# First expert pass in blocks of 128 neighbouring rows, its map built inside the pass, low parts of the tokens subtracted by VectorE inside it

## The chip, the cores and the metric

One core of one Trainium2 chip. The time is device microseconds of one execution of the whole program; a run is compared by its median over several executions. Before the change it is 1549.99 us, the median of 3 runs from 1548.42 to 1551.87.

## What is computed

A trunk of two layers on 512 tokens of width 1024, in f32. Each layer runs a token mixer (layer 0 a Conformer convolution module of 31 taps, layer 1 a short gated convolution of 3 taps) and then a hierarchical mixture of experts. Each of the two sub-layers is wrapped as

```
h = x * (1 + scale(c)) + shift(c)
x = LayerNorm(ALPHA * x + (1 + gate(c)) * sublayer(h))
```

with scale, shift and gate from a matrix product of a conditioning vector c. The mixture of experts chooses for each token one of 4 groups and in it the best 2 of 8 experts, and sums their weighted outputs; an expert is

```
hid = silu(x @ w_gate) * (x @ w_up)        # 1024 -> 512
y   = hid @ w_down                         # 512 -> 1024
```

There are 32 experts a layer, 6 MB of weights each. The choice needs full f32 precision, so the mixers' products are made of a high part and a low part of each operand (`mm3`: high by high, high by low, low by high).

## The kernel before, in words

**Weights.** All large weights come through a ring of 6 SBUF tiles of 2 MB (`R`, `RING`), in the order of the list `todo`. `pump` issues the next tile's DMAs on SyncE's queue, `unit()` hands out the oldest tile, and `done()` gives one back and pumps; a tile's DMAs wait on the chip until the instructions that read its predecessor are through. The expert weights follow each other by pass; the numbers of the experts of pass 1 and later are read from `ids`, which the routing writes. Pass 0 uses experts 0 and 1 whatever the routing says, so its weights can come ahead of it.

**Passes.** Layer i's experts run in 14 passes (`PASSES`), each with 128 token slots, split among 1 to 4 experts; pass 0 has two experts with 64 slots each. In a pass (from L1239's loop) `t` runs over 16 steps: step t multiplies 128 rows of the gathered tokens, block k, with the gate (z = 0) or the up weights (z = 1). Before, four blocks of the gate come first, then four of the up, and again. After steps 3, 7, 11 and 15 `release` gives tiles back. Then come `silu`, the product, a transposition, and eight steps with the down weights. f32 matmuls show as two instructions each.

**Gather.** Tokens reach their slots by a matmul with a one-hot matrix (`gather`, L1005 for pass 0, L1011 for the later ones). It makes two blocks k at a time; ScalarE evicts the even one and VectorE the odd one (L1014, L1016), with the map of the adaLN scale and shift (`affe`, `offe`) in the same instruction. `u_pass` gives partition p the rows 8p to 8p + 7 of a weight matrix, in two halves of four rows (runs of 8 KB). So block k of a pass consists of the columns k, k + 8, k + 16, ... of X: a step of eight elements. For pass 0 the gather reads X itself with that step as its weights. For the later passes it reads `nh` and `nl`, the high and the low parts of X in the permuted order, which are made just after the router's logits (L933, by `split`): ScalarE copies each of the four blocks of 128 tokens to `nh` (L461), and GpSimd subtracts for `nl` (L462).

**The permuted map.** `affine` (L443 to L445) makes `aff` and `off`, 128 neighbouring channels a column. `fold_router` adds the router's bias from `off` (L254), and builds the map in the order of the passes, `aff8`: an iota on GpSimd (L259), seven small instructions on VectorE (L260 to L266), eight matmuls (L269) and a copy on ScalarE (L272). Its inner `finish` adds the bias to `rb` and scales the router's weights `rw` (L275, L276). It is called in both mixers ahead of the output product: in layer 0 between the convolution's moments (`moments`, L722, L725) and their use (L816 to L822, spread over all channels by L831, applied in `conv_norm`, L839, L840); in layer 1 after the last weight product of the mixer and before the output product, whose weights `Out.fold` scales on GpSimd (L531) and splits on ScalarE and VectorE (L533, L539).

**Order.** The schedule is written by hand: each engine runs its instructions in the order of the program text, GpSimd too, and waits only for data and buffers. `W` hands out one of 21 tiles of 2 KB a partition, `P` one of 8 PSUM banks in three groups ("a" 4, "b" 2, "c" 2). Between the router's logits (L891) and pass 0 VectorE chooses the experts (`choose`, L905 to L923: a round of five steps for the group and the best expert together, then a round for the second best), TensorE counts (L938 to L946), and the ranks, the places and the one-hot of pass 0 follow (L950 to L1060). `flex` and, in layer 0, `side_ada` are modulation products whose last steps stand in this stretch and at step 3 of pass 0 (L366, L381, L384, L389).

Of the kernel before, what the change touches and what calls it, by code (L numbers as in the profile page):

```python
# [62 lines left out]
def trunk_kernel(ctx: ExitStack, tc: tile.TileContext, x, c, ada_w, ada_b, a_w_in, a_b_in, a_w_dw, a_b_dw,  # L63
# [114 lines left out]

    def u_last(i, d):
        def f():  # L180
            n = len(PASSES[-1])
            t = R([128, n, 2, 512])
            for s, e in enumerate(experts(i, NP - 1)):
                nc.sync.dma_start(t[:, s], e_w_down[i, e].rearrange("o (p h k) n -> h p (o k) n", h=2, k=2)
                                  [1][:, :, d * 512:(d + 1) * 512])
            return t
        return f
# [9 lines left out]
    for i in range(DEPTH):  # L197
        if i == 1:
            todo += [u_bin(nb) for nb in range(2)]
            for nb in range(2, KD):  # L200
                todo += [u_ada1(1, 1 + nb // 2, nb % 2), u_bin(nb)]
        else:
            todo += [rest.popleft()]
        todo += [u_out((a_w_out, b_w_out)[i][0], h) for h in range(2)]
        todo += list(rest) if i == 0 else []
        todo += [u_ada1(1, v, kq) for v in ((1, 0), (5,))[i] for kq in range(2)]
        for g in range(NP):
            n = len(PASSES[g])
            if g < NP - 1:
                todo += [u_pass(i, g, j) for j in range(3 * n)]  # L210
            else:
                todo += [u_pass(i, g, j) for j in range(5 * n // 2)] + [u_last(i, d) for d in range(2)]
# [38 lines left out]
    def fold_router(i, rw, aff, off):  # L251
# [3 lines left out]

        u, spread8 = W([128, 512]), W([128, KD, 2, 8])
# [11 lines left out]
        for k in range(KD):  # L268
            PE.matmul(p[:, 64:80], div8[:, 112 - 16 * k:240 - 16 * k], spread8[:, k].rearrange("p z j -> p (z j)"),  # L269
                      start=k == 0, stop=k == KD - 1)  # L270
        aff8[i] = T([128, 2, 8], F32, "aff8")
        S.activation(aff8[i].rearrange("p z j -> p (z j)"), p[:, 64:80], AF.Copy)  # L272

        def finish():
            V.tensor_add(rb[:, i, :], rb[:, i, :], p[:, :NG + NE])  # L275
            V.tensor_mul(rw, rw, bc(aff[:, :, None], [128, KD, NG + NE]))  # L276
# [34 lines left out]
    aff8 = {}  # L311
# [540 lines left out]
    for i in range(DEPTH):  # L852
# [77 lines left out]

        for q in range(NQ):
            qs = slice(q * 128, (q + 1) * 128)
            split(nh[:, :, qs], nl[:, :, qs], X[:, q, :].rearrange("p (n k) -> p k n", k=KD), G)  # L933
# [65 lines left out]
        def gather(Q, k0):  # L999
            p = P("c", (128, 2, 256))  # L1000
            n = 128 if Q % (NP // 2) == 0 else 256
            for k in (k0, k0 + 1):
                for q in range(NQ):
                    if Q == 0:
                        PE.matmul(p[:, k - k0, :n], X[:, q].rearrange("p (n k) -> p k n", k=KD)[:, k], oh(Q, q), start=q == 0, stop=q == NQ - 1)  # L1005
                        continue
# [3 lines left out]
                    for part, src in enumerate((nh, nl)):  # L1010
                        PE.matmul(p[:, k - k0], src[:, k, q * 128:(q + 1) * 128], o, start=q == 0 and part == 0,  # L1011
                                  stop=q == NQ - 1 and part == 1)
            k = k0
# [4 lines left out]
        affe, offe = aff8[i][:, 0], aff8[i][:, 1]  # L1018
# [106 lines left out]
        def block(e, rest, eid, tiles):  # L1125
# [6 lines left out]
            for h, xt in enumerate((xa, xb)):  # L1132
# [8 lines left out]
                for b in range(4):  # L1141
                    PE.transpose(p[:, b, :], xt[:, b * 128:(b + 1) * 128], ident)
                for b in range(4):
# [62 lines left out]
        for g, kind in enumerate(PASSES):  # L1206
# [27 lines left out]
            for t in range(2 * KD):  # L1234
                z, k = t // 4 % 2, t // 8 * 4 + t % 4
                if t % 4 == 0:
                    w = [piece(t // 4 * ns + s) for s in range(ns)]
                for s, a, b in cols:
                    PE.matmul(pgu[z][a:b, :], xe(Q, k, j)[:, a:b], w[s][:, t % 4, :], start=k == 0, stop=k == KD - 1)  # L1239
# [12 lines left out]
                if g == 0:  # L1252
                    if t in (0, 4, 6):
                        gather(0, {0: 2, 4: 4, 6: 6}[t])
# [276 lines left out]
```

## Time and profile before

| what | value |
| --- | --- |
| median of 3 runs | 1549.99 us |
| profiled execution, its own time | 1551.05 us |
| its span in the trace | 1548.9 us |
| TensorE busy | 1431.8 us, 92% |
| weight loads of TensorE (beside matmuls) | 785.4 us, 51% |
| VectorE busy | 726.0 us, 47% |
| ScalarE busy | 341.4 us, 22% |
| GpSimd busy | 283.9 us, 18% |
| DMA of the ring's queue | 486.82 MB, 79.2% of 16 engines |
| mean rate from HBM | 314 GB/s over the span |

Matmuls overlap each other in the pipeline, so a busy TensorE is not one at its peak. Layer 0's mixer ends at about 265 us, its experts at about 767 us; layer 1's mixer ends at about 1010 us. In the rows further down PE is TensorE, PEld its weight loads, DVE VectorE, ACT ScalarE, POOL GpSimd and SPq SyncE's queue of DMAs; L12 is line 12 of the kernel before.

### The profile page before, as it was taken

To read this page: it belongs to the slowest core of one execution; us is meant where nothing else is said; L and a number is where in the kernel's file an instruction comes from. 1 tells how busy PE (TensorE), PEld (TensorE's weight loads), DVE (VectorE), ACT (ScalarE), POOL (GpSimd) and SP (SyncE) were. 2 spreads that over 40 slices of the span, in tenths; PEclk is the share of its full clock that TensorE was granted. 3 is DMA by queue.
4 is the path that set the end of the run, shared out by engine and by line. 5 is a ranking of instruction groups with operands and counts; after the bars stand their busy time and mean duration, and the time that the engine had idled before them with its cause. 6 is when DMAs were issued, how large, how long until landed. Compare 5 with 4: busy or idle time off the path is not lost. (4 is left out here: it accounts for less than half of the span.)

```text
span 1548.9 us, 21328 instructions
## 1 busy us (share of the span) xinstructions
PE 1431.8 (92%) x8424; PEld 785.4 (51%) x8424; DVE 726.0 (47%) x1290; ACT 341.4 (22%) x583; POOL 283.9 (18%) x283
## 2 busy tenths in 40 slices
PE   5999888798999999998899898979899999999975
PEld 3444467553545444543277776856354444445422
DVE  2799887442333333333157876552433333333214
ACT  1456365120011101101052222232110111001001
POOL 1399923223000000000024105020500000000002
PEclk8999989899999999999899998989999999999988
DMA  8954424489999999999994673237999999999984
GB/s 296 396 184 169 161 88 184 164 313 422 421 394 403 389 421 421 421 420 418 360 303 150 196 243 131 101 123 304 365 422 415 407 405 400 421 421 420 420 358 172
DMA packets 112453, 488.73 MB, mean 316 GB/s; under 512 B 11971, under 2 KB 45259, under 8 KB 63179
## 3 DMA queue, kind: packets, MB, share of 16 engines
q1 hardware_dynamic: 108043, 486.82, 79.2%
q8 instruction: 71, 1.16, 0.3%
q0 software_dynamic: 128, 0.04, 0.2%
q10 hardware_dynamic: 4160, 0.30, 0.2%
q14 instruction: 51, 0.42, 0.1%
HBM read 485.02 MB, written 2.10 MB: 314 GB/s over the span
## 5 line engine op out<-in xcount | busy, mean ns | idle before, releaser
L1239 PE MATMUL pa<-ring,w 128*32 128x512 f32 (+2 forms) x2624 | 433.2, 607 | 25.8 <-DMA ring<-in_e_w_up_dram 12.1
L1239 PEld LDWEIGHTS pa<-ring,w 128*32 128x32 f32 (+2 forms) x2624 | 119.2, 120 | 275.7 <-issue 244.6
L1113 DVE TENSOR_TENSOR X<-X,pb 128x512 f32<-128x512 f32 x208 | 133.8, 683 | 265.8 <-PE pb L1121 259.5
L1305 PE MATMUL pa<-ring,w 128*32 128x512 f32 (+2 forms) x1312 | 207.8, 601 | 6.5 <-DMA ring<-in_e_w_down_dram 4.9
L1121 PE MATMUL pb<-w,w 128*128 128x512 f32 x416 | 128.0, 428 | 0.0
L1305 PEld LDWEIGHTS pa<-ring,w 128*32 128x32 f32 (+2 forms) x1312 | 60.6, 120 | 130.4 <-issue 114.2
L746 PE MATMUL pa<-RB,ring 128*128 128x512 f32 x256 | 117.1, 615 | 6.2 <-DMA ring<-in_a_w_in_dram 4.1
L1121 PEld LDWEIGHTS pb<-w,w 128*128 128x128 f32 x416 | 70.8, 189 | 96.5 <-issue 83.0
L1325 DVE SCALAR_TENSOR_TENSOR w<-pa,ws,w 128x512 f32<-128x512 f32 x56 | 41.9, 750 | 160.1 <-PE pa L1305 157.5
L691 POOL TENSOR_TENSOR w<-w,w 128x512 f32<-128x512 f32 x80 | 104.7, 1309 | 57.1 <-ACT w L689 51.5
L1096 ACT ACTIVATE w<-pc 128x512 fp32r<-128x512 f32 x28 | 16.7, 597 | 431.4 <-PE pc L1093 431.4
L1011 PE MATMUL pc<-w,RB 128*128 128x256 f32 x448 | 111.3, 288 | 0.0
L1011 PE MATMUL pc<-w,RC 128*128 128x256 f32 x448 | 108.5, 278 | 0.0
L1016 DVE TENSOR_SCALAR w<-pc,aff 128x256 f32<-128x256 f32 (+1 forms) x64 | 32.7, 511 | 126.1 <-ACT w L1014 126.1
L462 POOL TENSOR_TENSOR RC<-w,RB 128x512 fp32r<-128x512 f32 x8 | 10.9, 1382 | 440.0 <-ACT RB L461 440.0
L1011 PEld LDWEIGHTS pc<-w,RB 128*128 128x128 f32 x448 | 84.5, 189 | 2.7 <-issue 1.6
L1011 PEld LDWEIGHTS pc<-w,RC 128*128 128x128 f32 x448 | 84.1, 188 | 1.1
L746 PEld LDWEIGHTS pa<-RB,ring 128*128 128x128 f32 x256 | 49.3, 197 | 69.1 <-issue 63.5
L1014 ACT ACTIVATE w<-pc,aff 128x256 f32<-128x256 f32 (+1 forms) x64 | 34.4, 537 | 224.1 <-PE pc L1011 184.0
L705 DVE SCALAR_TENSOR_TENSOR pb<-RC,w,pb 128x512 f32<-128x512 f32 x126 | 83.6, 746 | 0.0
L1366 POOL TENSOR_TENSOR X<-X,w 128x512 f32<-128x512 f32 x3 | 4.9, 1620 | 428.6 <-ACT X L1365 428.6
L461 ACT ACTIVATE w<-w 128x512 fp32r<-128x512 f32 x58 | 36.5, 630 | 205.8 <-DVE w L1325 205.7
(348 smaller groups left out, 1911.2 us busy)
## 6 DMA issues: line engine op xcount, KB each, us to landing
ring<-in_e_w_gate_dram SPq DMA_DIRECT2D x128, 1024.0 KB, 12.1
ring<-in_e_w_up_dram SPq DMA_DIRECT2D x128, 1024.0 KB, 15.8
ring<-in_e_w_down_dram SPq DMA_DIRECT2D x120, 1024.0 KB, 15.9
ring<-in_ada_w_dram SPq DMA_DIRECT2D x14, 2048.0 KB, 11.6
ring<-in_ada_w_dram SPq DMA_DIRECT2D x10, 1536.0 KB, 6.4
ring<-in_b_w_in_dram SPq DMA_DIRECT2D x24, 512.0 KB, 6.4
ring<-in_a_w_in_dram SPq DMA_DIRECT2D x8, 1024.0 KB, 8.1
ring<-in_e_w_down_dram SPq DMA_DIRECT2D x16, 512.0 KB, 13.8
```

The costliest lines, as they stand in the source:

```text
L461: S.activation(hi, x, AF.Copy)
L691: G.tensor_add(vp, vp, z)
L705: V.scalar_tensor_tensor(t if j == TAPS - 1 else acc[n % 2], a, wj, acc[n % 2], op0=OP.mult, op1=OP.add)
L746: PE.matmul(p, w[:, k, h, s], hT[:, k, :], start=k == 0, stop=k == KD - 1)
L1011: PE.matmul(p[:, k - k0], src[:, k, q * 128:(q + 1) * 128], o, start=q == 0 and part == 0, stop=q == NQ - 1 and part == 1)
L1014: S.activation(xe(Q, k), p[:, 0, :n], AF.Identity, bias=offe[:, k:k + 1], scale=affe[:, k:k + 1])
L1016: V.tensor_scalar(xe(Q, k), p[:, 1, :n], affe[:, k:k + 1], offe[:, k:k + 1], op0=OP.mult, op1=OP.add)
L1113: V.tensor_add(half(q, d), half(q, d), p)
L1121: PE.matmul(p, C[:, q * 128:(q + 1) * 128], ys[d][z], start=z == 0, stop=z == 1)
L1239: PE.matmul(pgu[z][a:b, :], xe(Q, k, j)[:, a:b], w[s][:, t % 4, :], start=k == 0, stop=k == KD - 1)
L1305: PE.matmul(pd[d][a:b, :], hT[:, (2 * u + f) * 128 + a:(2 * u + f) * 128 + b], w[s][d][:, f, :], start=u + f == 0, stop=u + f == 2)
L1325: V.scalar_tensor_tensor(ys[d], pd[d], ws, GF[d], op0=OP.mult, op1=OP.mult)
```

## The change

Pass 0 takes its rows in blocks of 128 neighbouring channels: the gather reads X[:, q, 128k : 128k + 128], the map of pass 0 is `aff`, `off` themselves, and the new `u_first` loads four ring tiles, each with two blocks of the gate and up weights of both experts, in four DMAs of 512 KB in runs of 2 KB. Steps of pass 0 alternate between gate and up (z = t % 2, k = t // 2). Its later gathers stand at steps 1, 5 and 9 instead of 0, 4 and 6. The permuted map leaves `fold_router` for a function of its own, `by_rows`, called at step 3 of pass 0; its matmuls and its copy follow at step 13. After the logits only ScalarE's copies to `nh` remain; the subtractions for `nl` go to VectorE, one each at steps 2, 4, 6 and 8. The later passes keep their order of rows.

```
                 nc.sync.dma_start(t[:, y], w.rearrange("o (p h k) n -> h p (o k n)", h=2, k=2 if z == 2 else 4)[h])
+            return t
+        return f
+
+
+    def u_first(i, u):
+        def f():
+            t = R([128, 2, 2, 2, 512])
+            for s, e in enumerate(experts(i, 0)):
+                for z, w in enumerate((e_w_gate, e_w_up)):
+                    nc.sync.dma_start(t[:, s, :, z], w[i, e, u * 256:(u + 1) * 256, :]
+                                      .rearrange("o (k p) n -> p (o k) n", p=128))
             return t
...
             n = len(PASSES[g])
-            if g < NP - 1:
+            if g == 0:
+                todo += [u_first(i, u) for u in range(4)] + [u_pass(i, g, 4 + u) for u in range(2)]
+            elif g < NP - 1:
                 todo += [u_pass(i, g, j) for j in range(3 * n)]
...
+        def finish():
+            V.tensor_add(rb[:, i, :], rb[:, i, :], p[:, :NG + NE])
+            V.tensor_mul(rw, rw, bc(aff[:, :, None], [128, KD, NG + NE]))
+        return finish
+
+
+    def by_rows(aff, off):
         u, spread8 = W([128, 512]), W([128, KD, 2, 8])
...
                             op=OP.mult)
-        for k in range(KD):
-            PE.matmul(p[:, 64:80], div8[:, 112 - 16 * k:240 - 16 * k], spread8[:, k].rearrange("p z j -> p (z j)"),
-                      start=k == 0, stop=k == KD - 1)
-        aff8[i] = T([128, 2, 8], F32, "aff8")
-        S.activation(aff8[i].rearrange("p z j -> p (z j)"), p[:, 64:80], AF.Copy)
         def finish():
-            V.tensor_add(rb[:, i, :], rb[:, i, :], p[:, :NG + NE])
-            V.tensor_mul(rw, rw, bc(aff[:, :, None], [128, KD, NG + NE]))
+            p = P("b")
+            for k in range(KD):
+                PE.matmul(p[:, :16], div8[:, 112 - 16 * k:240 - 16 * k], spread8[:, k].rearrange("p z j -> p (z j)"),
+                          start=k == 0, stop=k == KD - 1)
+            r = T([128, 2, 8], F32, "aff8")
+            S.activation(r.rearrange("p z j -> p (z j)"), p[:, :16], AF.Copy)
+            return r
         return finish
...
     V.tensor_scalar(ecol[:, 3:4], ecol[:, 0:1], 2.0, 0.0, op0=OP.subtract, op1=OP.min)
-    aff8 = {}
     rank = T([NE, NE], BF, "rank")
...
+
+        def tokens(q):
+            qs = slice(q * 128, (q + 1) * 128)
+            return nh[:, :, qs], nl[:, :, qs], X[:, q, :].rearrange("p (n k) -> p k n", k=KD)
+
+        def tokens_low(q):
+            hi, lo, x = tokens(q)
+            V.tensor_sub(lo, x, hi.bitcast(F32))
+
         for q in range(NQ):
-            qs = slice(q * 128, (q + 1) * 128)
-            split(nh[:, :, qs], nl[:, :, qs], X[:, q, :].rearrange("p (n k) -> p k n", k=KD), G)
+            hi, lo, x = tokens(q)
+            S.activation(hi, x, AF.Copy)
...
                     if Q == 0:
-                        PE.matmul(p[:, k - k0, :n], X[:, q].rearrange("p (n k) -> p k n", k=KD)[:, k], oh(Q, q), start=q == 0, stop=q == NQ - 1)
+                        PE.matmul(p[:, k - k0, :n], X[:, q, k * 128:(k + 1) * 128], oh(Q, q), start=q == 0, stop=q == NQ - 1)
                         continue
...
                                   stop=q == NQ - 1 and part == 1)
+            affe, offe = maps[min(Q, 1)]
             k = k0
...
-        affe, offe = aff8[i][:, 0], aff8[i][:, 1]
+        maps = [(aff, off)]
...
                     PE.transpose(p[:, b, :], xt[:, b * 128:(b + 1) * 128], ident)
+                affe, offe = maps[1]
                 for b in range(4):
...
             for t in range(2 * KD):
-                z, k = t // 4 % 2, t // 8 * 4 + t % 4
-                if t % 4 == 0:
+                z, k = (t % 2, t // 2) if g == 0 else (t // 4 % 2, t // 8 * 4 + t % 4)
+                if t % 4 == 0 and g == 0:
+                    tiles.append(unit())
+                elif t % 4 == 0:
                     w = [piece(t // 4 * ns + s) for s in range(ns)]
                 for s, a, b in cols:
-                    PE.matmul(pgu[z][a:b, :], xe(Q, k, j)[:, a:b], w[s][:, t % 4, :], start=k == 0, stop=k == KD - 1)
+                    PE.matmul(pgu[z][a:b, :], xe(Q, k, j)[:, a:b],
+                              w[s][:, t % 4, :] if g else tiles[-1][:, s, k % 2, z, :],
+                              start=k == 0, stop=k == KD - 1)
                 if t % 4 == 3:
...
                 if g == 0:
-                    if t in (0, 4, 6):
-                        gather(0, {0: 2, 4: 4, 6: 6}[t])
+                    if t in (1, 5, 9):
+                        gather(0, t // 4 * 2 + 2)
+                    if t in (2, 4, 6, 8):
+                        tokens_low(t // 2 - 1)
+                    if t == 3:
+                        rows8 = by_rows(aff, off)
+                    elif t == 13:
+                        r = rows8()
+                        maps.append((r[:, 0], r[:, 1]))
                     if t == 3:
...
                         if i == 0:
```

## Rows read from the trace of the kernel before

**Rows 1.** The table by stages of layer 0, one line a stretch of the span; columns: from:to us, length, then busy us (and instructions) of PE, PEld, DVE, ACT and POOL, the granted clock of TensorE as a share of full speed, the busy share of the DMA engines, GB/s.

```profile
197.50:230.00 32.50, 31.93 (x158) 25.05 (x158) 27.87 (x39) 22.58 (x39) 9.97 (x6) 0.92 0.22 76
...
269.00:282.00 13.00, 3.33 (x64) 1.73 (x56) 12.72 (x19) 4.59 (x4) 9.84 (x4) 0.72 0.92 367
...
282.00:297.00 15.00, 14.31 (x82) 11.01 (x82) 5.96 (x28) 3.26 (x7) 0.00 (x0) 0.79 0.02 9
...
297.00:318.00 21.00, 21.00 (x97) 12.68 (x96) 4.01 (x13) 2.79 (x4) 0.00 (x0) 1.00 0.61 229
...
400.00:500.00 100.00, 100.00 (x604) 50.00 (x604) 37.04 (x71) 11.36 (x20) 0.00 (x0) 1.00 0.98 404
```

**Rows 2.** SyncE's queue in order of time around the start of layer 0's experts; start us, us from the first to the last issue of the line, line, operation, tile and tensor, count.

```profile
263.90 0.81 SPq L174 DMA_DIRECT2D ring<-in_e_w_up_dram  x2
...
297.46 13.35 SPq L174 DMA_DIRECT2D ring<-in_e_w_gate_dram  x4
...
343.07 2.28 SPq L174 DMA_DIRECT2D ring<-in_e_w_up_dram  x4
```

**Rows 3.** The timeline from the logits to the counts in layer 0 (lines of POOL, DVE and PE); start us, us, engine, line, operation, out<-in, shape, count, and in brackets the idle time before and what ended it.

```profile
267.37 11.48 POOL L462 TENSOR_TENSOR RC<-X,RB 128x1024 fp32r<-128x1024 f32 x4 [21.08 <-ACT RB L461]
...
268.67 3.66 PE L366 MATMUL pc<-ring,w 128*32 128x256 f32 x64
...
269.07 0.36 DVE L905 TENSOR_REDUCE w<-w 128x16 f32<-128x128 f32 x2
...
269.39 3.84 DVE L907 TENSOR_TENSOR w<-w 128x128 f32<-128x128 f32 x2
...
273.15 5.72 DVE L909 TENSOR_TENSOR w<-w,rev 128x128 f32<-128x128 f32 x2
...
279.76 0.29 DVE L905 TENSOR_REDUCE w<-w 128x16 f32<-128x128 f32 x1
...
281.37 0.29 DVE L922 TENSOR_TENSOR r_O<-w,w 128x128 bf16<-128x128 f32 x1
...
282.05 0.29 PE L938 MATMUL pb<-r_O,ones_b 128*128 128x32 bf16 x4 [9.72 <-DVE r_O L923]
```

**Rows 4.** The timeline at the same place in layer 1, the first matmul of the counts.

```profile
1027.22 0.29 PE L938 MATMUL pb<-r_O,ones_b 128*128 128x32 bf16 x4 [9.72 <-DVE r_O L923]
```

**Rows 5.** Groups of instructions by line, shapes kept apart; the first line from the stretch 258 to 285 us, the others from the whole span; columns: line, engine, operation, out<-in, shape, count | busy us, mean ns of one | idle us before.

```profile
L891 PE MATMUL pa<-w,w 128*128 128x108 f32 x64 | 7.4, 274 | 0.0
...
L462 DVE TENSOR_TENSOR w<-w,w 128x512 fp32r<-128x512 f32 x58 | 39.7, 687 | 3.7 <-ACT w L461 2.4
...
L461 ACT ACTIVATE w<-w 128x512 fp32r<-128x512 f32 x58 | 36.5, 630 | 205.8 <-DVE w L1325 205.7
...
L461 ACT ACTIVATE RB<-X 128x1024 fp32r<-128x1024 f32 x8 | 16.2, 2106 | 0.0
...
L462 POOL TENSOR_TENSOR RC<-X,RB 128x1024 fp32r<-128x1024 f32 x8 | 23.0, 2907 | 84.3 <-ACT RB L461 84.3
```

**Rows 6.** The timeline of TensorE in pass 0 of layer 0 (two gathers, two runs of gate/up steps).

```profile
284.39 4.08 PE L1005 MATMUL pc<-w,X 128*128 128x128 f32 x16
...
290.62 4.07 PE L1005 MATMUL pc<-w,X 128*128 128x128 f32 x16
...
294.62 2.79 PE L1239 MATMUL pa<-ring,w 128*64 128x512 f32 x12
...
308.83 7.95 PE L1239 MATMUL pa<-ring,w 128*64 128x512 f32 x36
```

**Rows 7.** The timeline of layer 0 between the moments and the normalisation of the convolution.

```profile
184.84 2.68 PE L254 MATMUL pb<-w,affB 128*128 128x36 f32 x16 [0.32 <-DVE affB L445]
...
191.45 3.60 PE L269 MATMUL pb<-w,w 128*128 128x16 f32 x16 [3.93 <-DVE w L266]
...
195.16 0.27 ACT L816 ACTIVATE w<-pc 128x128 f32<-128x128 f32 x1
...
201.32 0.69 DVE L840 TENSOR_TENSOR w<-w,pa 128x512 f32<-128x512 f32 x1 [1.02 <-PE pa L831]
```

**Rows 8.** The timeline of layer 1 ahead of the output product; the two lines of POOL from that engine's own timeline.

```profile
927.93 0.42 POOL L259 IOTA w<- 128x240 f32 x1 [68.98 <-PE pa L466]
...
928.33 21.04 POOL L531 TENSOR_TENSOR ring<-ring,w 128x512 f32<-128x512 f32 x16
...
941.80 1.21 DVE L443 TENSOR_TENSOR affA<-colP,mods 128x8 f32<-128x8 f32 x1
...
945.59 1.95 PE L254 MATMUL pb<-w,affB 128*128 128x36 f32 x16
...
954.63 0.19 DVE L275 TENSOR_TENSOR rb<-rb,pb 128x36 f32<-128x36 f32 x1 [3.90 <-ACT aff L272]
...
957.54 0.67 PE L467 MATMUL pb<-w,w 128*128 128x512 f32 x1
```

**Rows 9.** The table by stretches of 4 us in layer 1's mixer, columns as in rows 1; the first stretch lies in GpSimd's burst of 16 instructions from 833 to 859 us.

```profile
852.00:856.00 4.00, 0.00 (x0) 0.00 (x0) 4.00 (x3) 0.63 (x1) 3.92 (x4) 0.87 0.08 17
...
956.00:960.00 4.00, 3.48 (x8) 2.61 (x9) 3.96 (x8) 4.00 (x9) 0.00 (x0) 0.50 0.00 0
```

**Rows 10.** DMA issues on the page: tile and tensor, engine, operation, count, KB each, median us from issue to landing.

```profile
ring<-in_a_w_in_dram SPq DMA_DIRECT2D x8, 1024.0 KB, 8.1
```

## The prediction

> **What bounds the kernel now.** I read the stage table first [rows 1]. From 400 us on TensorE is busy all the time and the DMA engines at 0.98: the expert passes run with both full, so nothing short of taking work out makes a pass itself shorter. Between the router and the second pass the picture is another: the DMA share is 0.02 in 282 to 297 us and 0.61 in the next stretch. There the ring is full, and nothing is fetched until pass 0 gives a tile back. The SyncE queue [rows 2] shows the moment: the first weights of pass 1 are issued at 297.46 us, 0.05 us behind the end of pass 0's fourth step (294.62 + 2.79 us [rows 6]). So the start of the weight stream, and with it the end of the layer's experts, hangs on how soon pass 0 gets through its steps. What is won there is kept: later issues (343.07 us, in pass 1) are released by the same TensorE order, and with 39% of their time to spare in 297 to 318 us the DMA engines can follow an earlier demand.
>
> Ahead of pass 0 I read the timeline around the choice of experts [rows 3]. GpSimd subtracts the low parts from 267.37 us, four instructions in 11.48 us. VectorE starts choosing at 269.07 us; its pairs of L907 and L909 take 3.84 and 5.72 us. Once GpSimd is through, one such instruction takes 0.29 us, and the second round of five, from 279.76 us, is over at 281.37. TensorE waits 9.72 us for the choice. Layer 1 shows the same 9.72 us [rows 4].
>
> **Low parts out of the choice.** From the start of the first round to that of the second it is 10.69 us (269.07 to 279.76); five undisturbed steps and the one between the rounds, at 0.32 us each, are 1.9 us. So the choice ends 8.8 us sooner in each layer, all of it on the path, as TensorE waits for it. What is late next is TensorE: its matmuls before the wait end at 272.33 us (268.67 + 3.66), 1 us before the new time. As it then hardly idles, I expect its clock to stay up; in the table it is 0.72 and 0.79 of full speed on either side of 282 us, after the wait. That gives 0.3 us more on the small matmuls of the counts. Bounds: 6 us (one or two steps still held) to 9.1 us.
>
> **Neighbouring rows as weights of the gather.** A gather of pass 0 issues 16 matmul instructions whose weights are X with a step of eight elements. They take 4.08 us at 284.39, just behind the wait, and 4.07 us at 290.62 [rows 6], 0.25 us each either way: the pace does not follow the clock, so I hold the stepped weight load for what sets it. The logits' matmuls, f32 and 128x128 too but packed, take 7.4 us for 64, 0.116 each [rows 5]; for 128 columns instead of 108 I take 0.125. So 2.0 us a gather, and with four of them 8.0 us a layer less. All four lie between the choice and the end of the gate/up part, on TensorE. Bounds: 0 (the step is not the cause) to 8.3 us. Gates and ups now alternate by step; the same 64 instructions remain, at 7.95 us for 36 [rows 6], and each gather after the first has two steps behind it on TensorE before its rows are wanted: nothing.
>
> **What pass 0 gets.** The permuted map's eight matmuls, 16 instructions, stand ahead of the last two steps, on TensorE's path: 0.116 each, 1.9 us (upper bound 3.6 us, their time now [rows 7]). The map's seven VectorE instructions, some 2 us, and the iota come at step 3 beside matmuls; without that cover they cost those 2 us. Four subtractions of 1024 elements go to VectorE at steps 2, 4, 6 and 8. No row shows VectorE with a step of eight. Packed, 512 elements take 0.69 us, so 1.3; ScalarE's copy with this step takes 2.1 us where 512 packed ones take 0.63 [rows 5], 1.7 times as long per element; GpSimd needs 2.9. I take 2.2, by ScalarE's factor, bounds 1.3 to 2.9. Behind them on VectorE stand the odd evictions of the gathers, wanted two steps or more later, and in layer 0 the last additions of two modulations, whose PSUM buffer the second next gather wants: it starts 1.2 us late. In layer 1, with one such tile less, it doesn't. With 1.3 us there is no wait in either layer, with 2.9 it is 1.9. The Trainium skill, SBUF — State Buffer, section "SBUF: two separate sides" (under "Door 1"), notes that an access crossing into a new 16-byte line pays a penalty; with a step of 32 bytes that speaks against giving this work to VectorE. By that rule the 1.2 us stand, by the packed row alone the sum would be 1.2 us better.
>
> Route and pass 0 together: 8.8 + 0.3 + 8.0 - 1.9 - 1.2 = 14.0 us in layer 0, 15.2 us in layer 1.
>
> **Shorter pieces.** Pass 0's gates and ups come in 16 DMAs of 512 KB in runs of 2 KB, for 8 of 1 MB in runs of 8 KB: eight more issues on SyncE's queue, which waits for releases at that time. DMAs of 1 MB in runs of 1 KB land in 8.1 us [rows 10], so a 2 MB tile takes 16 us at most; the last of them is issued at 263.90 us now [rows 2] and wanted at the twelfth step, over 30 us later in the new order too. Nothing; without that cover up to 16 us.
>
> **The map out of the mixers.** Layer 0 [rows 7]: TensorE stands from 187.52 to 191.45 us for the spread map and works on it for 3.60 us; ScalarE's copy of it waits, and behind that the square of the mean (195.16 us), from which it is 6.16 us to L840 (201.32 us). The map goes. In its place GpSimd's additions start 0.3 us sooner and catch the three small instructions of `affine`: in layer 1 one such takes 1.21 us under GpSimd [rows 8], so they end about 187.1 us, and TensorE's copy of the router bias and the chain to L840 start there. With the same 6.16 us (some of its steps fall under GpSimd, its 16 matmuls get a higher clock) L840 starts at 193.3, 8.0 us sooner; bounds 6 to 10, by whether GpSimd holds all or none. From there to 230 us TensorE is busy 31.93 of 32.50 us with what this chain feeds [rows 1], so it is kept.
>
> Layer 1 [rows 8]: without the map the router's bias ends on TensorE at 947.54 (945.59 + 1.95). Now VectorE adds it at 954.63, and the first product with all it needs runs at 957.54, 2.9 us on. The same 2.9 us from 947.6 make it 950.5, 7.0 us sooner; and the product's next 3 us, at half clock now (0.50, 1.2 GHz [rows 9]), lose 1.4 us less. Against that: GpSimd's folds of the output weights stood behind the map's iota, which waited 68.98 us for its tile. They now start when their weights have landed, and fall among VectorE's splits of the layer's weights. The earlier GpSimd burst of 16 instructions left TensorE without work for 4 us [rows 9]; part of the new one falls on an idle VectorE, so I take 2, bounds 0 and 4. Net 6.4 us, bounds 4.4 to 8.4.
>
> **Sum.** 8.0 + 14.0 + 6.4 + 15.2 = 43.6 us off the profiled execution's own 1551.05 us (span 1548.9, 2.15 around it): 1507.4. That execution stood 1.1 us over the median of the runs, 1549.99; so 1506 us.
>
> **Rivals.**
> The step is not the price: the 16 us of the gathers stay, 1522 us. For it: the loads of X are the only stepped ones, so no second row shows the effect. Against: equal times behind the wait and later. Chance 0.10.
> Layer 1's mixer loses: GpSimd, freed of the iota's wait, holds VectorE's splits for 16 instructions of 1.3 us, 21 us, and TensorE waits as long: 8.4 - 21 = -12.6 us there for 6.4, 1525 us. For it: the 4 us hole. Against: VectorE idles between its bursts. Chance 0.08.
> Hidden anyway: TensorE's full passes eat the earlier start of the weight stream, and only the mixers' 14.4 us remain, 1536 us. Against: TensorE enters pass 1 sooner by as much as the stream. Chance 0.04.
> Slower: VectorE becomes the bound of pass 0. From step 2 TensorE has 14 steps of 0.88 us, three gathers of 2.0, the map's 1.9 and 0.7 of transposes, 21 us; VectorE has 4.0 us of old work (297 to 318 us [rows 1]), 2 for the map and the subtractions. From 3.8 us a subtraction on, four times the excess lies on the path; at 9.3 us it eats the 22 us of a layer, and at 10 us the time is 1506 + 2 x 4 x 6.2 = 1556 us. GpSimd's 2.9 speaks against it. Chance 0.03.
> That the subtractions or the map stay where they are in the queues, and nothing changes (1550 us), I give 0.02.
>
> **Numbers.** The forecast keeps 0.73. By the bounds of its terms it lies between 1500 us (10 + 15.8 + 15.8 + 8.4 off) and 1517 (6 + 10.5 + 12.4 + 4.4 off). The range also takes in the first two rivals: 1497 to 1528 us. About 0.2% (3 us) is what a measurement of this kernel can tell from no change: faster by more 0.95, within it 0.02, slower 0.03.
>
> **What would show it.** Right: no GpSimd subtraction between the logits and pass 0; pairs of L907 and L909 at some 0.35 us; a wait of TensorE for the choice near 1 us; gathers of pass 0 at 2.0 us; subtractions in pass 0 at 2.2 us; the first weights of pass 1 issued 20 us sooner in layer 0; no map between the moments and the normalisation. Wrong: gathers still at 4 us, TensorE idle behind VectorE in pass 0, or holes among layer 1's weight products.

## The result, and the profile after

The changed kernel takes 1515.8 us (median of 4, 1512.3 to 1518.3) where the kernel before took 1550.9 beside it (median of 4, 1548.4 to 1552.5): ratio 0.9773, 95% interval 0.9749 to 0.9797. The profiled execution has a span of 1513.7 us, 35.2 less than before. The forecast was 1506 us, 43.6 us less. The mechanism came out; 8.4 us by the spans, 9.8 by the medians, did not.

First the table by stages of layer 0, columns as in [rows 1], the stretches moved to where the same work now lies.

```profile
261.00:267.40 6.40, 4.72 (x86) 2.67 (x78) 5.17 (x24) 4.51 (x4) 0.00 (x0) 1.00 0.92 332
267.40:272.20 4.80, 4.73 (x28) 4.45 (x28) 1.37 (x10) 2.01 (x4) 0.00 (x0) 0.64 1.02 430
272.20:296.20 24.00, 23.13 (x136) 11.92 (x132) 16.24 (x40) 2.90 (x8) 0.00 (x0) 1.00 0.73 275
```

The stretch of the choice is half as long and POOL is empty in it. VectorE now has 16.24 us of work in pass 0, and TensorE is still busy 23.13 of 24 us there. The second line shows that the granted clock is only 0.64 behind the choice.

The timeline from the choice to the map in layer 0 (columns as in [rows 3, 6]):

```profile
261.06 0.36 DVE L924 TENSOR_REDUCE w<-w 128x16 f32<-128x128 f32 x2
261.38 0.38 DVE L926 TENSOR_TENSOR w<-w 128x128 f32<-128x128 f32 x2
261.70 0.38 DVE L928 TENSOR_TENSOR w<-w,rev 128x128 f32<-128x128 f32 x2
...
263.01 0.29 DVE L924 TENSOR_REDUCE w<-w 128x16 f32<-128x128 f32 x1
...
265.30 0.27 PE L966 MATMUL pb<-r_O,ones_b 128*128 128x32 bf16 x4 [0.98 <-DVE r_O L942]
...
267.47 3.30 PE L1033 MATMUL pc<-w,X 128*128 128x128 f32 x16
...
274.11 2.05 PE L1033 MATMUL pc<-w,X 128*128 128x128 f32 x16
...
281.35 2.05 PE L1033 MATMUL pc<-w,X 128*128 128x128 f32 x16 [0.87 <-DVE mods L403]
...
292.48 1.96 PE L292 MATMUL pb<-w,w 128*128 128x16 f32 x16
```

The pairs that took 3.84 and 5.72 us [rows 3] take 0.38 each, and TensorE waits 0.98 us for the choice instead of 9.72. From the second gather on a gather takes 2.05 us for 4.07 [rows 6]; the first takes 3.30, in the stretch with the low clock. The first pass 1 weights move with it on SyncE's queue, for [rows 2]:

```profile
278.07 8.10 SPq L174 DMA_DIRECT2D ring<-in_e_w_gate_dram  x4
...
322.69 2.01 SPq L174 DMA_DIRECT2D ring<-in_e_w_up_dram  x4
```

They are issued at 278.07 us for 297.46 and 322.69 for 343.07, 19.4 and 20.4 us sooner. In layer 1's mixer it looks different. The timeline there, for [rows 8]:

```profile
880.78 11.30 POOL L550 TENSOR_TENSOR ring<-ring,w 128x512 f32<-128x512 f32 x8 [42.29 <-DMA ring<-in_b_w_out_dram]
...
887.47 7.15 DVE L424 SCALAR_TENSOR_TENSOR ring<-ring,cact 128x512 f32<-128x512 f32 x6
...
894.54 3.69 DVE L481 TENSOR_TENSOR w<-ring,w 128x512 fp32r<-128x512 f32 x6
...
895.27 0.50 PE L486 MATMUL pa<-RB,w 128*128 128x512 f32 x1 [3.79 <-DVE w L481]
...
903.65 13.17 POOL L550 TENSOR_TENSOR ring<-ring,w 128x512 f32<-128x512 f32 x8 [11.57 <-DMA ring<-in_b_w_out_dram]
...
931.36 1.87 PE L267 MATMUL pb<-w,affB 128*128 128x36 f32 x16
```

GpSimd's folds start as soon as their weights have landed, 47.5 us sooner than before where the layer itself is 20 us sooner. VectorE's six modulation instructions beside them take 7.15 us (4.06 in the kernel before), the splits of the next weights stand behind these on its queue, and TensorE has a hole of 3.79 us. The last line is the router's bias, which stood at 945.59 us [rows 8]. The table in stretches of 4 us shows the hole and the clock behind it:

```profile
888.00:892.00 4.00, 3.49 (x16) 2.49 (x14) 4.00 (x3) 1.26 (x2) 4.00 (x3) 1.00 0.00 0
892.00:896.00 4.00, 0.72 (x3) 0.64 (x4) 4.00 (x7) 0.00 (x0) 0.08 (x1) 1.00 0.16 15
896.00:900.00 4.00, 4.00 (x13) 3.10 (x12) 3.86 (x7) 0.63 (x1) 0.00 (x0) 0.57 0.94 361
```

### The profile page after: what moved, and what is told of

Same layout as the page of the kernel before. It is cut to its first block, busy times and chain, and to the rows that moved or that the text cites. A ratio compares the mean times of both kernels' runs of the same rounds, so it can differ in the third digit from the quotient of the medians.

```text
span 1513.7 us, 21337 instructions
## 1 busy us (share of the span) xinstructions
PE 1416.6 (94%) x8424; PEld 769.3 (51%) x8424; DVE 725.2 (48%) x1298; ACT 341.3 (23%) x583; POOL 264.2 (17%) x275
## 5 line engine op out<-in xcount | busy, mean ns | idle before, releaser
L1271 PE MATMUL pa<-ring,w 128*32 128x512 f32 (+2 forms) x2624 | 430.6, 605 | 25.8 <-DMA ring<-in_e_w_up_dram 12.4
L1125 ACT ACTIVATE w<-pc 128x512 fp32r<-128x512 f32 x28 | 16.7, 597 | 429.6 <-PE pc L1122 429.6
L486 PE MATMUL pa<-RB,w 128*128 128x512 f32 x168 | 68.7, 409 | 8.8 <-DVE w L481 8.8
L1045 DVE TENSOR_SCALAR w<-pc,aff 128x256 f32<-128x256 f32 (+1 forms) x56 | 29.4, 525 | 91.3 <-ACT w L1043 91.3
## 6 DMA issues: line engine op xcount, KB each, us to landing
ring<-in_e_w_up_dram SPq DMA_DIRECT2D x120, 1024.0 KB, 16.7
```

The lines of the kernel that those rows point to most:

```text
L486: PE.matmul(p, al, bh, start=False, stop=stop)
L1045: V.tensor_scalar(xe(Q, k), p[:, 1, :n], affe[:, k:k + 1], offe[:, k:k + 1], op0=OP.mult, op1=OP.add)
```

## Experiments

My theory from this trace: the choice (8.7 us a layer), the packed weights of the gather and the map out of layer 0's mixer are worth what the working said. What is missing was lost in two places that the change itself opened: layer 1's mixer, where the folds run free, and the clock behind the choice. Differences below are against the changed kernel's 1515.8 us where nothing else is said; each ratio is to the kernel before on the same chip, where 0.9773 (0.9749 to 0.9797) is the changed kernel's.

**Low parts back beside the choice** (e1_low_back).

```diff
-            S.activation(hi, x, AF.Copy)
+            split(*tokens(q), G)
...
-                    if t in (2, 4, 6, 8):
-                        tokens_low(t // 2 - 1)
```

> One part of the change undone: GpSimd subtracts the low parts right behind ScalarE's copies again, beside the choice of experts; rows, weights and the map stay as in the changed kernel. Theory (VectorE's steps of the choice are held by GpSimd's subtractions, and TensorE waits for all of it): the pairs of the choice are back at about 4 and 6 us, the wait of TensorE near 9.7 us, +8.7 us in each layer; in layer 0 VectorE's 0.9 us wait at the third gather goes. The first gather stays at half clock either way. 1515.8 + 17.4 - 0.9 = 1532 us. Rival (the choice became quick because the map's instructions or something else left it, not the low parts): choice and time stay, 1516 us. Rival (the later start of the weight stream is caught up in the passes): 1518 us.

Measured: 1533.9 us, ratio 0.9884 (0.9868 to 0.9901), 18 us more. VectorE's choice and TensorE's wait in its timeline:

```profile
260.55 3.82 DVE L926 TENSOR_TENSOR w<-w 128x128 f32<-128x128 f32 x2
...
267.23 0.35 DVE L930 TENSOR_REDUCE w<-w 128x16 f32<-128x128 f32 x2
267.54 2.69 DVE L932 TENSOR_TENSOR w<-w,w 128x128 f32<-128x128 f32 x1
...
272.88 0.29 PE L965 MATMUL pb<-r_O,ones_b 128*128 128x32 bf16 x4 [9.39 <-DVE r_O L942]
```

The long pairs and the long wait are back; the choice is 8.4 us longer in each layer. Not every VectorE instruction is held: the two reductions at 267.23 us, amid GpSimd's subtractions (258.53 to 270.08 us), take 0.35 us together. Of the 18 us, 13.4 are there when layer 1's pass 1 starts. The rest comes later: from the issue of the last weights to that of the first output it takes 44.1 us for the changed kernel's 41.3, with TensorE's clock at 0.64 in 1485 to 1495 us, where the changed kernel has 1.00 in the same work. This part is worth about half of the change.

**Low parts alone, in the kernel before** (e2_low_alone).

```diff
-            split(nh[:, :, qs], nl[:, :, qs], X[:, q, :].rearrange("p (n k) -> p k n", k=KD), G)
+            S.activation(nh[:, :, qs], X[:, q, :].rearrange("p (n k) -> p k n", k=KD), AF.Copy)
...
+                    if t in (2, 4, 6, 8):
+                        tokens_low(t // 2 - 1)
```

> One part of the change alone in the kernel before: VectorE subtracts the low parts in pass 0 at steps 2, 4, 6 and 8; rows with a step of eight, the old weights and the map in the mixers stay. Theory: the choice gives 8.7 us in each layer, the four subtractions of 2.0 us lie beside stepped gathers that keep TensorE longer, so at most 0.9 us is lost in layer 0: 1550.9 - 17.4 + 0.9 = 1534 us. Rival (the parts need each other: with stepped gathers the earlier choice is lost to a wait of TensorE for VectorE in pass 0): above 1540 us.

Measured: 1534.6 us against 1551.3 before, ratio 0.9889 (0.9873 to 0.9906), 16.7 us less. From its timeline:

```profile
273.81 0.27 PE L942 MATMUL pb<-r_O,ones_b 128*128 128x32 bf16 x4 [0.98 <-DVE r_O L923]
```

TensorE waits 0.98 us for the choice, as in the changed kernel, and the gathers stay at 4.00 to 4.20 us. The part works without the others. From this side it comes to 16.7 us; the 18 us from the other side hold 4.7 that arose behind the start of layer 1's pass 1.

**Stepped weights of the gather alone** (e3_stepped).

```diff
-    PE.matmul(p[:, k - k0, :n], X[:, q, k * 128:(k + 1) * 128], oh(Q, q), ...)
+    PE.matmul(p[:, k - k0, :n], X[:, q].rearrange("p (n k) -> p k n", k=KD)[:, k], oh(Q, q), ...)
```

> Pass 0's gather alone reads its weights from X with a step of eight elements again, all else as in the changed kernel (what pass 0 computes is then not the reference's: rows and weights of its experts don't match). Theory (the stepped weight load sets the gather's pace, whatever the clock): each gather 4.07 us; three a layer were 2.05 us and the first 3.30 and 3.66 us, so +6.8 us in layer 0 and +6.5 us in layer 1, less up to 0.9 us of VectorE's wait that the longer gather hides: 1515.8 + 12.4 to 13.3 = 1528 to 1529 us. Rival of the prediction (the step is not the price; the gathers became short for another reason, as the order of the weights): 1516 us.

Measured: 1527.1 us, ratio 0.9838 (0.9821 to 0.9854), 11.3 us more by the medians and 13.8 by the profiled spans. Two gathers of layer 0 and the clock under the first one (timeline, then table by stretches of 2 us):

```profile
266.80 4.10 PE L1033 MATMUL pc<-w,X 128*128 128x128 f32 x16
...
273.91 4.07 PE L1033 MATMUL pc<-w,X 128*128 128x128 f32 x16
```

```profile
268.00:270.00 2.00, 2.00 (x10) 2.00 (x10) 0.00 (x0) 0.00 (x0) 0.00 (x0) 0.50 1.02 430
```

With stepped weights a gather takes the same time in a stretch mostly at half clock (0.50, 1.2 GHz) as at full: the load sets its pace. With packed ones it takes 2.05 us at full clock and 3.30 in the changed kernel's low stretch: there the clock counts. So the step is the price, and the rival that it is not falls. The 0.86 us wait for VectorE stayed, which I had given up to 0.9 us of cover.

**Folds of layer 1 held back** (e4_hold).

```diff
+        if i:
+            G.iota(W([128, 512])[:, :240], pattern=[[-8, 240]], base=0, channel_multiplier=1, **IOTA)
```

> In layer 1 GpSimd gets an iota back into a tile of the rotating pool that nobody reads, at the place where the kernel before had the map's; all else as in the changed kernel. Theory (the mixer of layer 1 lost 4.5 us of its 6.4 because GpSimd's folds ran among VectorE's weight splits from 880.8 us on and left TensorE without weights at 891 us): the folds wait again until the tile comes free, 28 to 45 us later, the hole of TensorE at 891 to 895 us and the half clock behind it go, and the time is 4.5 us less, 1511.3 us; bounds 2 and 6 us less. Rival (the hole is VectorE's own queue, its modulation work ahead of the splits, whatever GpSimd does): the hole stays, 1516 us. Rival (the folds lose as much wherever they fall): the hole moves to the later splits, 1516 us.

**No folds on GpSimd in layer 1** (e8_grow_late).

```diff
-                res = Out(grow, True)
+                res = Out(grow, False)
```

> Layer 1's output weights are not multiplied by the modulation on GpSimd any more; VectorE multiplies the product by it instead, as layer 0 does, eight instructions of 0.7 us in the last part of the mixer. All else as in the changed kernel. Theory (what layer 1's mixer lost, it lost to GpSimd's 16 folds): the hole of TensorE at 891 to 895 us goes, VectorE's splits run at 0.69 us; 6.2 us come back and 1.4 to 3 us go to VectorE's additional work behind the products, 1511 to 1512.6 us. Rival (VectorE's own modulation work makes the hole): the hole stays and the additional work comes on top, 1517 to 1521 us.

Measured: 1511.7 us, ratio 0.9740 (0.9724 to 0.9757), and 1510.4 us, ratio 0.9734 (0.9711 to 0.9756); 4.1 and 5.4 us less. These intervals overlap the changed kernel's, so the traces decide. GpSimd's timeline in the first and VectorE's modulation work there, then the stretch of the old hole in the first and in the second:

```profile
907.48 0.42 POOL L270 IOTA w<- 128x240 f32 x1 [69.10 <-PE pa L488]
907.86 21.07 POOL L553 TENSOR_TENSOR ring<-ring,w 128x512 f32<-128x512 f32 x16
```

```profile
886.32 4.06 DVE L427 SCALAR_TENSOR_TENSOR ring<-ring,cact 128x512 f32<-128x512 f32 x6
```

```profile
892.00:896.00 4.00, 4.00 (x19) 3.26 (x18) 3.83 (x7) 0.63 (x1) 0.00 (x0) 1.00 0.98 373
```

```profile
892.00:896.00 4.00, 4.00 (x19) 3.23 (x18) 3.77 (x6) 1.12 (x2) 0.00 (x0) 1.00 1.00 397
```

TensorE is full in both where it had 0.72 of 4 us. VectorE still has the same six modulation instructions, now in 4.06 us for 7.15, so it is GpSimd beside it that made the hole. The router's bias behind the weight loop starts at 925.1 and 924.3 us for 931.4; with what these executions were ahead where the mixer first waits for its splits (835.6 and 835.4 for 835.7) taken off, that is 6.1 and 6.7 us sooner, the loss in full. Some is given back at the product: at the choice 4.4 and 5.3 us are left, 1.7 less with the folds held until then, 1.4 less with VectorE's eight multiplications. Behind the choice both runs gain 1.6 us at a full clock in layer 1's first gather and lose 2.3 in its passes.

**The map back in the mixers** (e5_map_back).

```diff
+        r = by_rows(aff, off, p[:, 64:80])()
+        aff8[i] = r[:, 0], r[:, 1]
...
-                    if t == 3:
-                        rows8 = by_rows(aff, off)
-                    elif t == 13:
-                        ...
```

> The other part undone: the map for passes 1 on is made in the mixers again, where the kernel before made it (its iota, its seven VectorE instructions and its matmuls); rows, weights and low parts as in the changed kernel. Theory (in layer 0 the map was worth 8.0 us, in layer 1 only 1.9, because its iota also held GpSimd's folds back; in pass 0 it costs 1.96 us of matmuls a layer and with its VectorE instructions the 0.9 us wait in layer 0): +8.0 + 1.9 - 3.9 - 0.9 = +5.1, 1521 us. Rival (the prediction's price for layer 1, 6.4 us): 1525.5 us. Rival (the map was hidden in the mixers): 1511 us.

Measured: 1518.0 us (1516.5 to 1525.3), ratio 0.9793 (0.9757 to 0.9829): 2.2 us more, not distinguishable from none by the times, where I had expected 5. The timeline of layer 0 between the moments and the normalisation, for [rows 7]:

```profile
191.75 3.59 PE L294 MATMUL pb<-w,w 128*128 128x16 f32 x16 [3.86 <-DVE w L289]
...
201.62 0.69 DVE L862 TENSOR_TENSOR w<-w,pa 128x512 f32<-128x512 f32 x1 [1.02 <-PE pa L853]
```

The old chain is there again, 8.9 us later than the changed kernel's 192.76, and 8.3 us arrive at the choice; of these 4.9 are left at the first gather for pass 1 (301.17 for 296.24), as expected. My 5.1 missed two things behind it. Up to the gather that starts at 380.69 us in the changed kernel, TensorE waits 3.2 us for DMA instead of 4.9, and there 3.0 us are left (383.73). And layer 1's first gather ran at full clock here, 2.05 us for 3.66. With the map back layer 1's mixer takes 1.7 us more, where the theory had 1.9 and the prediction's price 6.4.

**TensorE kept busy behind the choice** (e6_busy).

```diff
         cnt = P("b")
+        for _ in range(4):
+            PE.matmul(cnt[:, 128:512]..., ones_b, bc(ones_b[:, None, :], [128, 3, 128]), start=True, stop=True)
...
+        for _ in range(3):
+            PE.matmul(cntc[:, 128:512]..., ones_b, bc(ones_b[:, None, :], [128, 3, 128]), start=True, stop=True)
         flex.step(flex.n - 1).copy()
```

> TensorE gets seven more bf16 matmuls of 384 columns a layer, of ones, into a part of the counts' PSUM tiles that nobody reads: four in its wait for the choice, three in the wait behind the counts. All else as in the changed kernel. Theory (the clock falls to half behind the choice because TensorE stands in these two waits): the granted clock stays at 1.0 through the first gather, which takes 2.05 us for 3.30 and 3.66, and the matmuls behind it 1.07 for 1.41: 1.6 us less in layer 0, 2.0 in layer 1, 1512.2 us. Rival (the clock is lost for another reason, and the added matmuls change nothing or stand in front of the counts): 1516 to 1517 us.

Measured: 1511.2 us, ratio 0.9733 (0.9706 to 0.9761), 4.6 us less by the medians (the intervals overlap) and 2.8 by the profiled spans. The table by stretches of 2 us and the first gather:

```profile
266.00:268.00 2.00, 1.74 (x17) 0.98 (x13) 1.69 (x9) 0.36 (x2) 0.00 (x0) 1.00 0.99 414
268.00:270.00 2.00, 2.00 (x19) 1.88 (x18) 0.41 (x2) 0.69 (x2) 0.00 (x0) 1.00 1.03 434
```

```profile
267.50 2.05 PE L1039 MATMUL pc<-w,X 128*128 128x128 f32 x16
```

The clock stays at 1.00, the gather takes 2.05 us, and in layer 1 too (998.64 us, at clock 1.00). The counts start no later (265.35 for 265.30). From the counts to the first gather for pass 1 it is 1.6 us less in each layer (29.33 for 30.94 us, 28.18 for 29.80). So at these two places the low clock cost 3.2 us. In layer 0 the work in the waits is what keeps it up: with packed weights the first gather there took 2.90 to 3.68 us in all eight traces without this work, and 2.05 in both with it. The 1.6 us of layer 0 did not last in this execution: at layer 1's choice nothing of them is left (992.25 for 991.89 us), as the clock was 0.66 in 930 to 940 us of its mixer for 1.00. In layer 1 the same work proves less, and what decides without it I can't say: in four other runs (e4_hold, e5_map_back, e8_grow_late, e11_low_packed) layer 1's first gather ran at full clock with the same waits of 0.98 and 0.65 us.

**Low parts in pass 0 on GpSimd** (e7_low_pool), and the same made to wait (e10_pool_late); the last two lines of the edit are in the second alone.

```diff
-            V.tensor_sub(lo, x, hi.bitcast(F32))
+            G.tensor_sub(lo, x, hi.bitcast(F32))
...
+                    if t == 2:
+                        G.tensor_copy(rest[:, 0:1], Vd[:, 0, 0:1])
```

> The low parts stay in pass 0, at the same steps, but GpSimd subtracts them instead of VectorE. All else as in the changed kernel. Theory (it is GpSimd beside VectorE that costs, not where in the order the work stands): GpSimd runs four instructions of 2.9 us and more, VectorE's evictions and its map in pass 0 are held by up to one of them each; TensorE waits for some: 2 to 5 us a layer more, about 1521 us. Rival (in pass 0 nobody waits for VectorE, and it is relieved of 8 us): 0.9 us less, 1515 us.

> GpSimd subtracts the low parts as in the run before with GpSimd, but has to wait: a copy of one column from the table that VectorE writes behind the first gather stands ahead of the subtractions on GpSimd's queue, so that they can't start before some 272 us. Theory (that run lost 16 us since GpSimd's queue was empty and took the subtractions beside the choice again, wherever they stand in the program): the choice is as quick as in the changed kernel, TensorE waits about 1 us for it, GpSimd runs from 272 to 284 us beside the evictions and the map of pass 0, and VectorE's instructions there are held by up to 2.9 us: 0 to 3 us a layer more, 1518 us. Rival (GpSimd is too slow for this work at any place): TensorE waits at the second pass for the low parts, 1526 us and more.

Measured: 1532.1 us, ratio 0.9868 (0.9843 to 0.9893), and 1532.7 us, ratio 0.9877 (0.9860 to 0.9894). Both of my sizes were wrong: 5 and 2 us expected, 16 and 17 measured. In the first, GpSimd and TensorE's wait:

```profile
258.37 2.91 POOL L957 TENSOR_TENSOR RC<-X,RB 128x1024 fp32r<-128x1024 f32 x1 [21.65 <-ACT RB L961]
...
261.54 8.63 POOL L957 TENSOR_TENSOR RC<-X,RB 128x1024 fp32r<-128x1024 f32 x3
...
272.73 0.29 PE L966 MATMUL pb<-r_O,ones_b 128*128 128x32 bf16 x4 [9.41 <-DVE r_O L942]
```

The subtractions ran beside the choice again, though the program has them in pass 0: nothing stands ahead of them on GpSimd's queue, so they start when their inputs are there. This is the same thing that set the folds of layer 1 free. In the second they wait, the choice is quick (TensorE waits 0.98 us), and the harm moves into pass 0:

```profile
274.27 8.45 POOL L957 TENSOR_TENSOR RC<-X,RB 128x1024 fp32r<-128x1024 f32 x3
...
274.62 2.52 DVE L1103 TENSOR_SCALAR w<-w 128x16 f32<-128x16 f32 x1
...
277.35 2.60 DVE L1105 TENSOR_TENSOR w<-w 128x16 f32<-128x16 f32 x1
279.98 2.77 DVE L1106 TENSOR_TENSOR w<-w 128x16 f32<-128x16 f32 x1
...
284.07 0.69 PE L400 MATMUL pc<-ident,w 128*128 128x128 f32 x2 [7.38 <-DVE w L1045]
```

An instruction of 16 elements, 0.11 to 0.18 us in the changed kernel, takes as long as what is left of GpSimd's subtraction. A short chain of them, which nobody is in a hurry for, holds the gather's eviction behind it, and TensorE waits 7.38 us. At both places tried it is the engine that costs; what helped was to give the work to another engine.

**VectorE's subtractions packed** (e11_low_packed).

```diff
-            V.tensor_sub(lo, x, hi.bitcast(F32))
+            V.tensor_sub(lo, X[:, q, :].rearrange("p (k n) -> p k n", k=KD), hi.bitcast(F32))
```

> VectorE's subtractions in pass 0 read the tokens packed instead of with a step of eight (the low parts then belong to other channels, so the output of passes 1 on is off by what they correct). All else as in the changed kernel. Theory (the step makes the subtraction 2.0 us; by the packed row it would be 1.3): 1.1 to 1.4 us each, and TensorE's 0.9 us wait for VectorE's modulation in layer 0 goes: 1515 us. Rival (the step costs VectorE nothing, and 2.0 us is the price of 1024 elements of two f32 inputs): 2.0 us each, wait and time as in the changed kernel.

Measured: 1512.7 us (1510.7 to 1519.9), ratio 0.9766 (0.9742 to 0.9791): no difference that the times can tell. The line of the subtraction in this run, then in the changed kernel (count: least/median/greatest ns, first and last start):

```profile
L957 DVE TENSOR_TENSOR RC<-X,RB x8: 1215/1216/1221, 276.2 to 1010.3; 128x1024 fp32r<-128x1024 f32 x8
```

```profile
L957 DVE TENSOR_TENSOR RC<-X,RB x8: 1993/2008/2023, 277.0 to 1016.5; 128x1024 fp32r<-128x1024 f32 x8
```

The step of eight makes it 2.01 us for 1.22, a factor of 1.65, and without it the third gather no longer waits for VectorE. On the path the price is the 0.87 us. The Trainium skill states that an access that crosses into a new 16-byte line pays a penalty (SBUF — State Buffer, "SBUF: two separate sides", under "Door 1"). The factor of 1.65 at a step of 32 bytes agrees.

**Both losses taken away** (e9_both): e8_grow_late and e6_busy in one.

> Two of the experiments together: the product of layer 1's mixer is multiplied by the modulation on VectorE (no folds on GpSimd), and TensorE gets the seven added matmuls a layer in its two waits behind the choice. Theory (the two losses are separate; of the second only layer 0's part is left, as the first gather of layer 1 ran at full clock already without the folds, and of layer 0's 1.6 us the end of its passes keeps 1.0): 1510.4 - 1 to 3 = 1507.5 to 1509.5 us. Rival (the added matmuls gain nothing once the folds are gone): 1510.5 us.

Measured: 1507.0 us (1504.2 to 1509.3), ratio 0.9709 (0.9692 to 0.9725), an interval below the changed kernel's. Its layer 0 keeps the clock at 1.00 behind the choice, and 892 to 896 us is full. It is the fastest of all and stands 1 us from the forecast: by the traces, what the forecast had too much is mostly these two losses. That it comes so close is in part luck: beside them its layer 0 passes gain 1.6 us against the changed kernel's and its layer 1 passes lose 2.3.

## Why the prediction was right, and where not

**The choice**: right. 8.74 us in layer 0 and 8.72 in layer 1 for 8.8; e1_low_back and e2_low_alone show GpSimd's subtraction as the cause, e10_pool_late that one VectorE instruction waits for one of GpSimd's. The Trainium skill says so (SBUF — State Buffer, "SBUF: two separate sides"): the pair of ports that the two share goes to one instruction for all of its time. The 2.5 to 2.8 us of 16 elements agree.

**The gathers**: the mechanism right, the first one of each layer mis-sized. Six of eight take 2.05 us for the 2.0 of the sum. The first takes 3.30 in layer 0 and 3.66 in layer 1 (last line below), for I expected the clock to stay up "As it then hardly idles". TensorE was busy 2.25 of 4 us from 264 to 268, and the clock fell at 268:

```profile
264.00:268.00 4.00, 2.25 (x34) 1.49 (x27) 2.87 (x13) 1.90 (x4) 0.00 (x0) 1.00 0.96 365
268.00:270.00 2.00, 2.00 (x12) 2.00 (x11) 0.38 (x2) 0.25 (x1) 0.00 (x0) 0.51 1.01 426
```

```profile
998.30 3.66 PE L1033 MATMUL pc<-w,X 128*128 128x128 f32 x16
```

I had also read [rows 1] too coarsely: the 0.79 of 282 to 297 us is a mean, and by stretches of 2 us the clock in the kernel before was 0.50 from 284 to 288, under its first gather:

```profile
284.00:286.00 2.00, 2.00 (x10) 1.83 (x9) 1.13 (x8) 0.75 (x2) 0.00 (x0) 0.50 0.03 8
286.00:288.00 2.00, 2.00 (x10) 2.00 (x10) 0.00 (x0) 0.00 (x0) 0.00 (x0) 0.50 0.00 0
```

That its 4.08 us equal the second's 4.07 showed that the stepped load hides the clock, not that a packed one would. The cost is 1.3 and 1.6 us in the gathers; from the counts to pass 1 e6_busy got 1.6 back in each layer.

**Pass 0's additions**: right. The map's matmuls took 1.96 us for 1.9, a subtraction 2.01 for 2.2; the wait in layer 0 was 0.87 for 1.2, and there was none in layer 1. The shorter pieces cost nothing, as forecast: TensorE waits for no DMA in pass 0 of either layer. Layer 0 from the choice to the first gather for pass 1 came to 12.4 us for 14.0; the 1.6 missing are the clock.

**The map out of layer 0's mixer**: right, 8.0 us at the choice for 8.0 (269.07 to 261.06), 8.3 us later again in e5_map_back.

**Kept through the passes**: right to 0.1 us in the changed kernel: 20.5 us at the first gather for pass 1, 20.4 at the fourth pass and at layer 1's first output weights (issued at 871.5 us for 891.9). "Hidden anyway" falls. Other runs show that it isn't exact. In e5_map_back 1.9 of 4.9 us were gone by 380 us; layer 1's passes took 2.3 us off the gains of e4_hold, e8_grow_late and e9_both, and put 4.7 on the loss of e1_low_back. Part of such shifts comes with other waits for DMA (3.2 us for 4.9 in e5_map_back), part in e1_low_back and e6_busy with a lower clock elsewhere; the rest stays open.

**Layer 1's mixer**: this step failed in its size. For the folds that were set free the prediction has "part of the new one falls on an idle VectorE, so I take 2, bounds 0 and 4"; measured were 6.2 us, outside these bounds. The layer arrived 20.4 us sooner, and the router's bias started only 14.2 us sooner (931.4 for 945.6). The burst is two bursts, each beside modulation work (six instructions in 7.15 us for 4.06, then eight in 10.58 for 5.38) with the next weights' splits behind it. The mixer gained 1.9 us for 6.4. The second rival's mechanism is thus real, at 6.2 us instead of its 21. e4_hold and e8_grow_late show it.

**Sum**: 8.0 + 12.4 + 1.9 + 12.9 (layer 1 from the choice on, forecast 15.2) = 35.2 us, the difference of the spans. Of the 8.4 missing, 4.5 are the mixer of layer 1 and 3.2 the clock; 0.7 is spread over pieces that I did not follow. Slower by VectorE did not happen, at 2.01 us a subtraction for the 3.8 from which it would have decided.

## What to carry to other kernels

A place in the program orders an instruction only against its own engine's queue; before an instruction is taken off a queue, look what stands behind it and was held by it, and what that will run into. GpSimd beside VectorE was paid for here by VectorE's shortest instructions, so work that both could do is worth trying on VectorE itself, at a place where nobody waits for VectorE. A mean clock over 15 us can hide that the instruction in question ran at half: read the clock under that instruction, and ask which limit the new form will meet.

## What the hardware showed that I had not expected

- A stepped f32 weight load (every eighth element) takes 0.25 us an instruction at 1.2 and at 2.4 GHz (4.08 us for 16 in the kernel before at 284.39 us, 4.07 at 290.62); packed, 0.13 at 2.4 GHz and 0.21 to 0.23 in a stretch that was mostly at half.
- The clock fell behind waits of only 0.98 and 0.65 us, and in layer 0 seven small matmuls in them kept it; with the same waits and without these it stayed up in layer 1 of four other runs. What tells these apart stays open.
- A VectorE instruction of 16 elements took up to 2.77 us beside GpSimd subtractions of 2.82; two reductions of 128 to 16 elements took 0.35 us together beside them (e1_low_back).
